# Feed-forward up projections as Strassen's seven block products, with the residual stream kept in DRAM meanwhile

## The chip, the cores and the metric

The kernel is one launch on one core of a Trainium2 chip. The metric is the device time of the launch in microseconds (us). A core has TensorE (PE in the profile, with its weight loads as PEld), VectorE (DVE), ScalarE (ACT), GpSimd (POOL) and SyncE (SP), which here issues nearly all DMAs. Each engine takes its instructions in the order in which they stand in its own queue; semaphores tie the queues together.

## The reference, cut to what matters

768 tokens (512 of one request, 256 of another) pass through two layers. Each layer is a mixer, a gated convolutional feed-forward and a gated embedding, each behind a root-mean-square norm and added to the residual `h`. The change is in the feed-forward:

```python
D_MODEL, D_FF, CONV_W = 1024, 2816, 3

def _rmsnorm(x, g):
    return x * lax.rsqrt(jnp.mean(x * x, axis=-1, keepdims=True) + EPS) * g

def _conv_ffn(x, w_up, conv_w, conv_b, w_down):
    u = x @ w_up                                   # (tokens, 2 * D_FF)
    up = jnp.pad(u, ((0, 0), (1, 1), (0, 0)))      # neighbours in the token direction
    u = up[:, :-2] * conv_w[0] + up[:, 1:-1] * conv_w[1] + up[:, 2:] * conv_w[2] + conv_b
    a, gate = jnp.split(u, 2, axis=-1)
    return (a * jax.nn.gelu(gate, approximate=False)) @ w_down

    # per layer l, in _trunk:
    h = h + _conv_ffn(_rmsnorm(h, norm_ffn_g[l]), ffn_w_up[l], ffn_conv_w[l], ffn_conv_b[l], ffn_w_down[l])
```

The arithmetic is float32.

## The kernel before

Features lie on the 128 partitions and tokens on the free axis. The residual is eight tiles `h0` to `h7` of 128 features by 768 tokens. A product of float32 quality is made of three float32r matmuls: weights and activations are each split into a high part and a low part (`whi`, `wlo`; `xh`, `xl`), and high by high, high by low and low by high are summed in PSUM (`gemm`, L78 to L85). Each of the three runs twice with the same weights, over the 512 tokens of one request and the 256 of the other.

Weights come in slabs of 128 x 1024 floats (512 KB), one for each 128 output features. `prep` (L58) loads a slab from DRAM on SP's queue (L66), makes the high part on ACT (L67) and the low part on DVE (L68). There are two buffers each of `raw`, `whi` and `wlo`, and `slab` keeps one slab ahead.

The feed-forward (`ffn`, L815) has 22 rounds j, one for each 128 of the 2816 features. A round has two projections (`proj`, L87), the value part and the gate part, of 24 pairs of matmuls each. DVE takes a projection out of PSUM and multiplies it by the norm's row factor `R` (L834), so the products run on the not yet normalized stream times the gain. Then the three taps of the convolution (ACT L838, DVE L839 and L841), the Gelu on ACT (L144), and the product into `act[j]` on DVE (L844). The first projection runs before `R` is there; the row sums follow it on PE (`proj0`, `norm_rows`). After the 22 rounds the down projection takes `act[j]` as its input (L131, L132, L85) and adds its sums to `h` (L865).

The order on each queue is made by the framework's scheduler from the order of the program and from priorities. Where a tile's buffer is used again, the new writer waits for the readers of the old.

## Time and profile before

| | |
|---|---|
| median of 3 runs | 2372.55 us (2371.6 to 2372.74) |
| span of the profiled execution | 2371.5 us |
| PE busy | 2347.3 us, 99% of the span |
| DVE busy | 1332.5 us, 56% |
| ACT busy | 918.7 us, 39% |
| POOL busy | 49.8 us, 2% |
| DVE's first L834 (round 0 of the first layer) | at 717.3 us |
| stretch of rounds 2 to 21 of the first layer in the rows below | 736.4 to 1072.2 us |

The profiled execution's span lies 1 us under the median, so the sums in span and the metric can be taken as one scale. PE's busy share alone does not say that PE is at its peak: matmuls overlap in it, and their ends are modelled. The distance from one start to the next is what counts. The idle time in a group's line is that of its engine, and what ended it.

### The profile page before, as it was taken

To read this page: it belongs to the slowest core of one execution; us is meant where nothing else is said; L and a number is where in the kernel's file an instruction comes from. 1 tells how busy PE (TensorE), PEld (TensorE's weight loads), DVE (VectorE), ACT (ScalarE), POOL (GpSimd) and SP (SyncE) were. 2 spreads that over 40 slices of the span, in tenths; PEclk is the share of its full clock that TensorE was granted. 3 is DMA by queue.
4 is the path that set the end of the run, shared out by engine and by line. 5 is a ranking of instruction groups with operands and counts; after the bars stand their busy time and mean duration, and the time that the engine had idled before them with its cause. 6 is when DMAs were issued, how large, how long until landed. Compare 5 with 4: busy or idle time off the path is not lost.

```text
span 2371.5 us, 32752 instructions
## 1 busy us (share of the span) xinstructions
PE 2347.3 (99%) x14004; PEld 2074.1 (87%) x14004; DVE 1332.5 (56%) x1814; ACT 918.7 (39%) x1190; POOL 49.8 (2%) x82
## 2 busy tenths in 40 slices
...
DMA packets 45616, 153.09 MB, mean 65 GB/s; under 512 B 5184, under 2 KB 7232, under 8 KB 45472
## 3 DMA queue, kind: packets, MB, share of 16 engines
...
q14 instruction: 34, 0.28, 0.0%
...
## 4 chain that ended last, share of the span: by engine, by line
PE 97%; DVE 1%; ACT 0%; issue 0%; DMA 0%; POOL 0%; SPq 0%; DVEq 0%
PE pj L85 76%; PE mm L85 11%; PE mm L249 4%; PE mm L331 2%; PE mm L692 1%; PE mm L299 1%; PE mm L235 1%; PE mm L553 0%; PE mm L609 0%; PE mm L685 0%; DVE y L934 0%; PE mm L212 0%; PE mm L290 0%; PE mm L344 0%; DMA xin<-xT 0%
## 5 line engine op out<-in xcount | busy, mean ns | idle before, releaser
L85 PE MATMUL pj<-xh,whi 128*128 128x512 f32 x3440 | 905.8, 344 | 8.9 <-ACT whi L67 5.8
L85 PE MATMUL pj<-xl,whi 128*128 128x512 f32 x3440 | 881.8, 337 | 2.5 <-DVE xl L138 2.4
L85 PE MATMUL pj<-xh,wlo 128*128 128x512 f32 x3440 | 879.4, 337 | 0.0
L85 PEld LDWEIGHTS pj<-xl,whi 128*128 128x128 f32 x3440 | 530.9, 188 | 80.7 <-DVE xl L138 4.6
L85 PEld LDWEIGHTS pj<-xh,whi 128*128 128x128 f32 x3440 | 527.6, 189 | 77.3 <-ACT whi L67 5.8
L85 PEld LDWEIGHTS pj<-xh,wlo 128*128 128x128 f32 x3440 | 525.8, 188 | 75.5
L67 ACT ACTIVATE whi<-raw 128x1024 fp32r<-128x1024 f32 (+1 forms) x244 | 255.8, 1048 | 761.0 <-PE pj L85 753.4
L68 DVE TENSOR_TENSOR wlo<-raw,whi 128x1024 fp32r<-128x1024 f32 (+1 forms) x244 | 296.8, 1216 | 139.2 <-ACT whi L67 139.1
L834 DVE TENSOR_TENSOR u<-pj,R 128x512 f32<-128x512 f32 (+1 forms) x176 | 90.1, 554 | 261.3 <-PE pj L85 261.1
L132 DVE TENSOR_TENSOR xl<-act,xh 128x770 fp32r<-128x770 f32 x88 | 83.5, 956 | 72.7 <-ACT xh L131 72.7
L131 ACT ACTIVATE xh<-act 128x770 fp32r<-128x770 f32 x88 | 73.7, 842 | 96.1 <-PE pj L85 96.1
L262 ACT COPY kc<-X 128x768 f32<-128x768 f32 x56 | 50.4, 900 | 124.5 <-PE mm L249 65.0
L85 PE MATMUL mm<-xh,whi 128*128 128x512 f32 x352 | 90.8, 339 | 0.0
L85 PE MATMUL mm<-xh,wlo 128*128 128x512 f32 x352 | 90.4, 338 | 0.0
L85 PE MATMUL mm<-xl,whi 128*128 128x512 f32 x352 | 90.4, 338 | 0.0
L249 PE MATMUL mm<-qc,kc 128*128 128x128 f32 x672 | 84.1, 275 | 0.0
L249 PEld LDWEIGHTS mm<-qc,kc 128*128 128x128 f32 x672 | 79.9, 192 | 2.2
L277 DVE COPY_PREDICATED A<-masks,mm 128x512 f32<-128x512 uint8 x112 | 60.4, 586 | 36.4 <-PE mm L249 36.3
L266 DVE TENSOR_TENSOR X<-X,F 128x768 f32<-128x768 f32 x56 | 53.4, 953 | 37.0 <-ACT qc L262 30.2
L144 ACT ACTIVATE cg<-cg 128x770 f32<-128x770 f32 x44 | 37.4, 849 | 89.1 <-DVE cg L841 89.1
L844 DVE TENSOR_TENSOR act<-act,cg 128x770 f32<-128x770 f32 x44 | 42.3, 961 | 38.5 <-ACT cg L144 38.5
L85 PEld LDWEIGHTS mm<-xh,whi 128*128 128x128 f32 x352 | 54.5, 189 | 7.5
...
## 6 DMA issues: line engine op xcount, KB each, us to landing
raw<-w_up SPq DMA_DIRECT2D x88, 512.0 KB, 3.5
raw<-w_ev SPq DMA_DIRECT2D x55, 512.0 KB, 3.5
raw<-w_dn SPq DMA_DIRECT2D x44, 512.0 KB, 3.5
raw<-w_od SPq DMA_DIRECT2D x24, 512.0 KB, 3.5
raw<-w_pg SPq DMA_DIRECT2D x16, 512.0 KB, 3.5
raw<-w_evo SPq DMA_DIRECT2D x8, 512.0 KB, 3.5
raw<-w_odo SPq DMA_DIRECT2D x8, 512.0 KB, 3.5
xin<-xT SPq DMA_DIRECT2D x8, 384.0 KB, 6.1
```

Of the source, the lines that this page charges most:

```text
L67: nc.scalar.activation(hi[:, s], raw[:, s], AF.Copy)
L68: nc.vector.tensor_tensor(out=lo[:, s], in0=raw[:, s], in1=hi[:, s].bitcast(F32), op=ALU.subtract)
L85: nc.tensor.matmul(o, w, x[:, c0:c0 + n], start=first and si == 0, stop=last and si == 2)
L131: nc.scalar.activation(xh[:, :n], src, AF.Copy)
L132: nc.vector.tensor_tensor(out=xl[:, :n], in0=src, in1=xh[:, :n].bitcast(F32), op=ALU.subtract)
L249: nc.tensor.matmul(p[:, j * 128:(j + 1) * 128], k[:, i * 128:(i + 1) * 128], q[:, i * 128:(i + 1) * 128], start=True, stop=True)
L262: nc.scalar.copy(dst.rearrange("p (n c j) -> p n c j", c=2, j=h), src)
L266: nc.vector.tensor_tensor(out=v1[:, :, 1, :], in0=v1[:, :, 1, :], in1=fv[:, :, 0, 0:1].to_broadcast([128, 2 * nb, h]), op=ALU.mult)
L277: nc.vector.copy_predicated(A[:, tl[0]:tl[0] + n, :], self.masks[:, li, :].unsqueeze(1).to_broadcast([128, n, 128]), p.rearrange("p (i t) ...
L331: nc.tensor.matmul(oo, l, r, start=n == 0, stop=n == len(mms) - 1)
L834: nc.vector.tensor_tensor(out=u[:, 1 + uc:1 + uc + w], in0=pj[:, c0:c0 + w], in1=self.R[:, c0:c0 + w], op=ALU.mult)
L844: nc.vector.tensor_tensor(out=act[j], in0=act[j], in1=c, op=ALU.mult)
```

## The change

The up projections of rounds 0 and 1 stay as they were (`NSTD` = 2). Each of rounds 2 to 21 is made of Strassen's seven block products in Winograd's form, with 15 block additions. The two by two blocks are: for the weights, input-feature tiles in pairs (k = 2p, 2p + 1) by value and gate part; for the tokens, the same pairs of feature tiles by two halves of the token axis. The token axis is 512 + 4 + 256 = 772 columns wide, with a gap of four zeros between the requests, so that a half is 386 columns (`HC`). The seven products run over four pairs p each, three float32r matmuls to a pair: 7 x 4 x 3 = 84 matmuls of 386 columns a round, against 96 (48 of 512 and 48 of 256 columns) before.

What comes with it:
- `prep_pair`: the weights of a round arrive in two loads of 512 KB, `ra` and `rb`, which take both `raw` buffers. S1 and S3 are made on POOL, S2 and S4 on DVE, and the high and low parts of A11 and A12, S2 and S1, S3 and S4, and A22 on ACT and DVE: 3584 columns to split a round, against 2048.
- `seven_operands`, four times, one for each pair of feature tiles, in rounds 0 and 1: the tokens are normalized on DVE (with `R`, so that a round's sums need no further factor), T1 and T2 are made on DVE, T3 and T4 on POOL, and seven high and low parts on ACT and DVE. Some of the parts are kept in the buffers of `h0` to `h7`.
- Hence `h` is written to DRAM ahead of the feed-forward, and read back for the sum with the down projection.
- `seven`: the products P1 to P7 go to three PSUM banks x, y and z; the sums are made on ACT (copies), DVE (additions out of PSUM) and POOL (`g`).
- `us` has two buffers instead of three, the gate's `c` one instead of two. The norm's `xh` and `xl` lie in buffers of `act`, and the order of the buffers in the down projection differs.

```diff
-UC = 1 + TP + 2 + TS + 1
-AC = TP + 2 + TS
-ACOL = ((0, TP), (TP + 2, TS))
+GAP = 4
+UC = 1 + TP + GAP + TS + 1
+AC = TP + GAP + TS
+HC = AC // 2
+NSTD = 2
...
+        if n == 2048:
+            self.ready.append(self.prep_pair(src))
+            return
         raw = self.wp.tile([128, 1024], F32, tag="raw", name="raw")
...
 
+    def prep_pair(self, src):
+        nc = self.nc
+        ra = self.wp.tile([128, 1024], F32, tag="raw", name="ra")
+        nc.sync.dma_start(out=ra, in_=src[:, 0:1024])
+        rb = self.wp.tile([128, 1024], F32, tag="raw", name="rb")
+        nc.sync.dma_start(out=rb, in_=src[:, 1024:2048])
+        a11, a12, a22, a21 = ra[:, 0:512], ra[:, 512:1024], rb[:, 0:512], rb[:, 512:1024]
+        def parts(hpool, htag, lpool, ltag, r):
+            n = r.shape[-1]
+            hi = hpool.tile([128, 1024], F32R, tag=htag, bufs=2, name=htag)[:, :n]
+            lo = lpool.tile([128, 1024], F32R, tag=ltag, bufs=2, name=ltag)[:, :n]
+            nc.scalar.activation(hi, r, AF.Copy)
+            nc.vector.tensor_tensor(out=lo, in0=r, in1=hi.bitcast(F32), op=ALU.subtract)
+            return [[(hi[:, c:c + 128], lo[:, c:c + 128]) for c in range(c0, c0 + 512, 128)]
+                    for c0 in range(0, n, 512)]
+        sa = self.fp.tile([128, 1024], F32, tag="S", bufs=2, name="sa")
+        sb = self.fp.tile([128, 1024], F32, tag="S", bufs=2, name="sb")
+        s2, s1, s3, s4 = sa[:, 0:512], sa[:, 512:1024], sb[:, 0:512], sb[:, 512:1024]
+        nc.gpsimd.tensor_tensor(out=s1, in0=a21, in1=a22, op=ALU.add)
+        nc.gpsimd.tensor_tensor(out=s3, in0=a11, in1=a21, op=ALU.subtract)
+        nc.vector.tensor_tensor(out=s2, in0=s1, in1=a11, op=ALU.subtract)
+        nc.vector.tensor_tensor(out=s4, in0=a12, in1=s2, op=ALU.subtract)
+        w = {}
+        w["A11"], w["A12"] = parts(self.wp, "whi", self.wp, "wlo", ra)
+        w["S2"], w["S1"] = parts(self.fp, "hs", self.fp, "ls", sa)
+        w["S3"], w["S4"] = parts(self.fp, "hs", self.fp, "ls", sb)
+        w["A22"], = parts(self.wp, "whi", self.wp, "wlo", rb[:, 0:512])
+        return w
+    def seven(self, X, c11, add):
+        nc = self.nc
+        W = self.slab()
+        x, y, z = None, None, None
+        def prod(bank, a, b, start):
+            for n, ((wh, wl), (xh, xl)) in enumerate(zip(W[a], X[b])):
+                for i, (w, v) in enumerate(((wh, xh), (wh, xl), (wl, xh))):
+                    nc.tensor.matmul(bank, w, v, start=start and n == 0 and i == 0, stop=n == 3 and i == 2,
+                                     skip_group_check=True)
+            self.tick()
+        pt = self.rp.tile([128, AC], F32, tag="Rt", name="p15")
+        ug = self.rp.tile([128, AC], F32, tag="sq", name="ug")
+        p1, p5, u2, g = pt[:, 0:HC], pt[:, HC:AC], ug[:, 0:HC], ug[:, HC:AC]
+        x = self.mm()[:, 0:HC]
+        prod(x, "A11", "B11", True)
+        nc.scalar.copy(p1, x)
+        y = self.mm()[:, 0:HC]
+        prod(y, "S2", "T2", True)
+        nc.vector.tensor_tensor(out=u2, in0=y, in1=p1, op=ALU.add)
+        z = self.mm()[:, 0:HC]
+        prod(z, "S1", "T1", True)
+        nc.scalar.copy(p5, z)
+        nc.gpsimd.tensor_tensor(out=g, in0=p1, in1=p5, op=ALU.add)
+        prod(x, "A12", "B21", False)
+        c11(x)
+        prod(y, "S3", "T3", False)
+        add(1, 1, y, g)
+        prod(z, "S4", "B22", False)
+        add(0, 1, z, u2)
+        prod(y, "A22", "T4", False)
+        add(1, 0, y, p1)
+    def seven_operands(self, x1, x2, ta, tb, slots):
+        nc = self.nc
+        b11, b12, b21, b22 = x1[:, 0:HC], x1[:, HC:AC], x2[:, 0:HC], x2[:, HC:AC]
+        t1, t2, t3, t4 = ta[:, 0:HC], ta[:, HC:AC], tb[:, 0:HC], tb[:, HC:AC]
+        nc.vector.tensor_tensor(out=t1, in0=b12, in1=b11, op=ALU.subtract)
+        nc.gpsimd.tensor_tensor(out=t3, in0=b22, in1=b12, op=ALU.subtract)
+        nc.vector.tensor_tensor(out=t2, in0=b22, in1=t1, op=ALU.subtract)
+        nc.gpsimd.tensor_tensor(out=t4, in0=b21, in1=t2, op=ALU.subtract)
+        s11, h2, l2, ha, la, hb, lb = slots
+        for hi, lo, v in ((s11[:, 0:HC], s11[:, HC:AC], b11), (ha, la, ta), (h2, l2, x2), (hb, lb, tb)):
+            nc.scalar.activation(hi, v, AF.Copy)
+            nc.vector.tensor_tensor(out=lo, in0=v, in1=hi.bitcast(F32), op=ALU.subtract)
+        self.X["B11"].append((s11[:, 0:HC], s11[:, HC:AC]))
+        for names, h, lo in ((("B21", "B22"), h2, l2), (("T1", "T2"), ha, la), (("T3", "T4"), hb, lb)):
+            self.X[names[0]].append((h[:, 0:HC], lo[:, 0:HC]))
+            self.X[names[1]].append((h[:, HC:AC], lo[:, HC:AC]))
...
     def ffn(self, l):
         nc, tc, a = self.nc, self.tc, self.a
-        with tc.tile_pool(name=f"f{l}", bufs=1) as fp:
+        with tc.tile_pool(name=f"f{l}", bufs=1) as fp, \
+                tc.tile_pool(name=f"hd{l}", bufs=1, space=bass.MemoryType.DRAM) as dp:
+            self.fp = fp
             conv = fp.tile([128, 2 * NF, 4], F32, tag="conv", name="conv")
             nc.sync.dma_start(out=conv, in_=a["conv"][l])
-            us = [fp.tile([128, UC], F32, tag=f"u{i}", name=f"u{i}") for i in range(3)]
-            self.norm_split(lambda k: self.h[k], C_FFN + 8 * l)
+            us = [fp.tile([128, UC], F32, tag=f"u{i}", name=f"u{i}") for i in range(2)]
+            def aslot(j, name, dt=F32R):
+                return fp.tile([128, AC], dt, tag=f"act{j}", name=name)
+            self.norm_split(lambda k: self.h[k], C_FFN + 8 * l, slot=lambda i, n: aslot(6 + i, n))
+            hd = dp.tile([KT, 128, T], F32, tag="hd", name="hd")
+            for k in range(KT):
+                nc.sync.dma_start(out=hd[k], in_=self.h[k])
             for u in us:
                 nc.gpsimd.memset(u[:, 0:1], 0.0)
-                nc.gpsimd.memset(u[:, 1 + TP:3 + TP], 0.0)
+                nc.gpsimd.memset(u[:, 1 + TP:1 + TP + GAP], 0.0)
                 nc.gpsimd.memset(u[:, UC - 1:UC], 0.0)
-            act = [fp.tile([128, AC], F32, tag=f"act{j}", name=f"act{j}") for j in range(NF)]
-            n = 0
-            for j in range(NF):
-                for part in range(2):
-                    pj = self.proj0(split=True) if n == 0 else self.proj()
-                    u = us[n % 3]
-                    n += 1
+            act = [None] * NF
+            self.X = {n: [] for n in ("B11", "B21", "B22", "T1", "T2", "T3", "T4")}
+            def operands(p):
+                x1, x2 = aslot(2, f"xn{2 * p}", F32), aslot(3, f"xn{2 * p + 1}", F32)
+                for k, x in ((2 * p, x1), (2 * p + 1, x2)):
+                    nc.gpsimd.memset(x[:, TP:TP + GAP], 0.0)
                     for (c0, w), (uc, _) in zip(CH, ACOL):
-                        nc.vector.tensor_tensor(out=u[:, 1 + uc:1 + uc + w], in0=pj[:, c0:c0 + w],
-                                                in1=self.R[:, c0:c0 + w], op=ALU.mult)
...
+                        nc.vector.scalar_tensor_tensor(out=x[:, uc:uc + w], in0=self.h[k][:, c0:c0 + w],
+                                                       scalar=self.cols[:, C_FFN + 8 * l + k:C_FFN + 8 * l + k + 1],
+                                                       in1=self.R[:, c0:c0 + w], op0=ALU.mult, op1=ALU.mult)
+                tags = [(self.xp, f"x{p}"), (fp, f"xb{p}")] + [(self.xp, f"x{4 + 3 * p + i}") for i in range(3)] \
+                    + [(self.hp, f"h{2 * p + i}") for i in range(2)]
+                self.seven_operands(x1, x2, aslot(4, "ta", F32), aslot(5, "tb", F32),
+                                    [pool.tile([128, AC], F32R, tag=t, name=t) for pool, t in tags])
+            def conv_taps(c, u, f):
...
+            def activate(j, u):
+                act[j] = aslot(j, f"act{j}", F32)
+                c = fp.tile([128, AC], F32, tag="c", name="cg")
+                conv_taps(act[j], u[0], j)
+                conv_taps(c, u[1], NF + j)
                 self.other(c, c, AF.Gelu)
                 nc.vector.tensor_tensor(out=act[j], in0=act[j], in1=c, op=ALU.mult)
+            for j in range(NSTD):
+                for part in range(2):
+                    n = 2 * j + part
+                    pj = self.proj0(split=True) if n == 0 else self.proj()
+                    for (c0, w), (uc, _) in zip(CH, ACOL):
+                        nc.vector.tensor_tensor(out=us[part][:, 1 + uc:1 + uc + w], in0=pj[:, c0:c0 + w],
+                                                in1=self.R[:, c0:c0 + w], op=ALU.mult)
+                    if part == 1:
+                        activate(j, us)
+                    operands(n)
+            for j in range(NSTD, NF):
+                u = us
+                def add(m, half, bank, other):
+                    o = u[m][:, 1 + half * HC:1 + (half + 1) * HC]
+                    nc.vector.tensor_tensor(out=o, in0=bank, in1=other, op=ALU.add)
+                    if half:
+                        nc.gpsimd.memset(u[m][:, 1 + TP:1 + TP + GAP], 0.0)
+                self.seven(self.X, lambda bank: nc.scalar.copy(u[0][:, 1:1 + HC], bank), add)
+                activate(j, u)
             self.use_lnexp()
             for ph in range(2):
                 accs = []
-                    xh, xl = self.split(j % 8, act[j])
+                    xh, xl = self.split((0, 1, 4, 5, 6, 7, 2, 3)[j % 8], act[j])
                     for m in range(4):
                         c = ((j % 2) * 4 + m) * 128
                         self.gemm(accs[m], hi[:, c:c + 128], lo[:, c:c + 128], xh, xl, ACOL, j == 0, j == NF - 1)
                 for m in range(4):
-                    h = self.h[ph * 4 + m]
+                    h = self.hp.tile([128, T], F32, tag=f"h{ph * 4 + m}", name=f"h{ph * 4 + m}")
+                    self.h[ph * 4 + m] = h
+                    nc.sync.dma_start(out=h, in_=hd[ph * 4 + m])
                     for o, (c0, w) in zip(accs[m], CH):
                         nc.vector.tensor_tensor(out=h[:, c0:c0 + w], in0=h[:, c0:c0 + w], in1=o, op=ALU.add)
                     self.square(ph * 4 + m, h)
 
...
-            for j in range(NF):
+            for j in range(NSTD):
                 r += [a["w_up"][l, j], a["w_up"][l, NF + j]]
+            r += [a["w_up2"][l, j] for j in range(NSTD, NF)]
```

How the queues stand. First DVE in a round in the middle of the up projections, before (two projections, value and gate part):

```order
L834 TENSOR_TENSOR u_5825<-pj,R 128x512
L834 TENSOR_TENSOR u_5825<-pj,R 128x256
L68 TENSOR_TENSOR wlo<-raw,whi 128x1024
L839 SCALAR_TENSOR_TENSOR act_5878<-u_5825,conv,act_5878 128x770
L841 SCALAR_TENSOR_TENSOR act_5878<-u_5825,conv,act_5878 128x770
L834 TENSOR_TENSOR u_5826<-pj,R 128x512
L834 TENSOR_TENSOR u_5826<-pj,R 128x256
L68 TENSOR_TENSOR wlo<-raw,whi 128x1024
L839 SCALAR_TENSOR_TENSOR cg<-u_5826,conv,cg 128x770
L841 SCALAR_TENSOR_TENSOR cg<-u_5826,conv,cg 128x770
L844 TENSOR_TENSOR act_5878<-act_5878,cg 128x770
```

The same place now, DVE in a round of seven products. `ug` holds P1 + P2 and then P1 + P5; `sa` is S2 and S1, `sb` S3 and S4 of the next round, `ls` their low parts, `ra` and `rb` the next round's raw weights, `mm` a PSUM bank, `u_5827` and `u_5828` the value and the gate part:

```order
L130 TENSOR_TENSOR ug<-mm,p_6576 128x386
L99 TENSOR_TENSOR sa<-sa,ra 128x512
L959 TENSOR_TENSOR act_6540<-act_6540,cg 128x772
L100 TENSOR_TENSOR sb<-ra,sa 128x512
L91 TENSOR_TENSOR ls<-sa,hs 128x1024
L91 TENSOR_TENSOR wlo<-ra,whi 128x1024
L975 TENSOR_TENSOR u_5828<-mm,ug 128x386
L975 TENSOR_TENSOR u_5827<-mm,ug 128x386
L91 TENSOR_TENSOR ls<-sb,hs 128x1024
L948 SCALAR_TENSOR_TENSOR act_6675<-u_5827,conv,act_6675 128x772
L91 TENSOR_TENSOR wlo<-rb,whi 128x512
L975 TENSOR_TENSOR u_5828<-mm,p_6576 128x386
```

Three taps (L950, L948, L950) follow and close the round: 15 instructions instead of 11, and the sums for PE's banks (L130, L975) now stand between the next round's weights.

POOL, which had nothing to do in the up projections, in a round of seven products:

```order
L97 TENSOR_TENSOR sa<-rb 128x512
L98 TENSOR_TENSOR sb<-ra,rb 128x512
L134 TENSOR_TENSOR ug<-p_6711 128x386
L977 MEMSET u_5828 128x4
L977 MEMSET u_5827 128x4
```

S1 and S3 of the next round, then g = P1 + P5 of this one, then the gaps.

DVE in the first layer's round 0, before, around the low part of the weights of the fourth projection (`wlo_6036`; `pj_5977` is the second projection):

```order
L834 TENSOR_TENSOR u0_5825<-pj_5897,R_5956 128x512
L834 TENSOR_TENSOR u0_5825<-pj_5897,R_5956 128x256
L839 SCALAR_TENSOR_TENSOR act0_5869<-u0_5825,conv_5823,act0_5869 128x770
L834 TENSOR_TENSOR u1_5826<-pj_5977,R_5956 128x512
L841 SCALAR_TENSOR_TENSOR act0_5869<-u0_5825,conv_5823,act0_5869 128x770
L834 TENSOR_TENSOR u1_5826<-pj_5977,R_5956 128x256
L68 TENSOR_TENSOR wlo_6036<-raw_6034,whi_6035 128x1024
```

And now: the same low part is `wlo_6080`, and 28 instructions stand between the first L965 (the former L834) and it; the last of them, it, and the next:

```order
L152 TENSOR_TENSOR ta_6057<-xn3_6050,ta_6057 128x386
L959 TENSOR_TENSOR act0_6039<-act0_6039,cg_6040 128x772
L157 TENSOR_TENSOR x7_6061<-xn3_6050,xb1_6060 128x772
L157 TENSOR_TENSOR x9_6063<-ta_6057,x8_6062 128x772
L157 TENSOR_TENSOR h3_6065<-tb_6058,h2_6064 128x772
L74 TENSOR_TENSOR wlo_6080<-raw_6078,whi_6079 128x1024
L965 TENSOR_TENSOR u0_5827<-pj_6084,R_5941 128x512
```

`xn` is a normalized pair of tiles, `ta` T1 and T2, `tb` T3 and T4; the L157 rows are low parts of operands of pairs 0 and 1. The low part moved from the 7th place behind `R` to the 30th. The operands of pairs 2 and 3 (rows of the same kind, and the first `prep_pair`) follow it.

## Rows read from the trace of the kernel before

**Rows 1.** The page's busy time by engine, share and instructions.

```profile
PE 2347.3 (99%) x14004; PEld 2074.1 (87%) x14004; DVE 1332.5 (56%) x1814; ACT 918.7 (39%) x1190; POOL 49.8 (2%) x82
```

**Rows 2.** The page's chain that ended last, by line.

```profile
PE pj L85 76%; PE mm L85 11%; PE mm L249 4%; PE mm L331 2%; PE mm L692 1%; PE mm L299 1%; PE mm L235 1%; PE mm L553 0%; PE mm L609 0%; PE mm L685 0%; DVE y L934 0%; PE mm L212 0%; PE mm L290 0%; PE mm L344 0%; DMA xin<-xT 0%
```

**Rows 3.** DVE by line, rounds 2 to 21, layer 0 (busy us, mean ns, idle before).

```profile
L68 DVE TENSOR_TENSOR wlo<-raw,whi 128x1024 fp32r<-128x1024 f32 x40 | 48.6, 1215 | 0.1
L834 DVE TENSOR_TENSOR u<-pj,R 128x512 f32<-128x512 f32 x80 | 40.9, 554 | 129.6 <-PE pj L85 129.6
```

**Rows 4.** DVE and ACT in order of time in mid-layer: start us, us, instruction, idle.

```profile
921.29 1.02 DVE L834 TENSOR_TENSOR u<-pj,R 128x512 f32<-128x512 f32 x2 [4.18 <-PE pj L85]
922.23 1.22 DVE L68 TENSOR_TENSOR wlo<-raw,whi 128x1024 fp32r<-128x1024 f32 x1
922.34 1.04 ACT L838 ACTIVATE cg<-u,conv 128x770 f32<-128x770 f32 x1 [0.28 <-DVE u L834]
...
938.06 1.02 DVE L834 TENSOR_TENSOR u<-pj,R 128x512 f32<-128x512 f32 x2 [4.18 <-PE pj L85]
```

**Rows 5.** PE in order of time where only 512-column matmuls follow each other.

```profile
2295.43 0.40 PE L85 MATMUL mm<-xh,ghi 128*128 128x512 f32 x1
...
2296.12 0.40 PE L85 MATMUL mm<-xh,ghi 128*128 128x512 f32 x1
```

**Rows 6.** DVE in order of time, instructions that do not wait for each other.

```profile
695.06 1.22 DVE L68 TENSOR_TENSOR wlo<-raw,whi 128x1024 fp32r<-128x1024 f32 x1
696.19 0.95 DVE L196 TENSOR_TENSOR acc<-acc,sq 128x768 f32<-128x768 f32 x1
697.06 5.66 DVE L138 SCALAR_TENSOR_TENSOR xl<-h,cols,xh 128x768 fp32r<-128x768 f32 x6
...
1069.54 2.70 DVE L132 TENSOR_TENSOR xl<-act,xh 128x770 fp32r<-128x770 f32 x3
```

**Rows 7.** DVE, then POOL, in order of time at the start; POOL alone later.

```profile
8.04 1.02 DVE L138 SCALAR_TENSOR_TENSOR xl<-xin,cols,xh 128x768 fp32r<-128x768 f32 x1 [1.20 <-ACT xh L137]
8.98 0.42 DVE L68 TENSOR_TENSOR wlo<-raw,whi 128x256 fp32r<-128x256 f32 x1
9.91 2.00 DVE L138 SCALAR_TENSOR_TENSOR xl<-xin,cols,xh 128x768 fp32r<-128x768 f32 x1 [0.52 <-ACT xh L137]
11.83 2.03 DVE L68 TENSOR_TENSOR wlo<-raw,whi 128x256 fp32r<-128x256 f32 x1
...
9.14 8.48 POOL L196 TENSOR_TENSOR acc<-acc,sq 128x768 f32<-128x768 f32 x4 [7.61 <-ACT sq L195]
...
43.00 1.85 POOL L471 TENSOR_TENSOR ks<-X 128x768 f32<-128x768 f32 x1 [25.37 <-DVE X L466]
```

**Rows 8.** DMA issues by line: count, KB each, us from issue to landing.

```profile
raw<-w_up SPq DMA_DIRECT2D x88, 512.0 KB, 3.5
...
hd<-h SPq DMA_DIRECT2D x8, 384.0 KB, 2.8
h<-hd SPq DMA_DIRECT2D x8, 384.0 KB, 3.5
```

**Rows 9.** ACT by line, rounds 2 to 21 of layer 0 (columns as in Rows 3).

```profile
L67 ACT ACTIVATE whi<-raw 128x1024 fp32r<-128x1024 f32 x41 | 43.5, 1062 | 180.4 <-PE pj L85 180.4
```

**Rows 10.** DVE, then ACT, in order of time, first rounds of layer 0.

```profile
716.19 0.96 DVE L169 TENSOR_TENSOR R<-R,Rt 128x768 f32<-128x768 f32 x1
...
719.67 1.06 ACT L67 ACTIVATE whi<-raw 128x1024 fp32r<-128x1024 f32 x1 [0.27 <-PE pj L85]
...
728.05 1.06 ACT L67 ACTIVATE whi<-raw 128x1024 fp32r<-128x1024 f32 x1 [1.54 <-PE pj L85]
```

**Rows 11.** Stretches at the start: us, busy us by engine, granted clock, DMA.

```profile
20.00:25.00 5.00, 5.00 (x17) 4.23 (x17) 5.00 (x6) 0.84 (x1) 0.00 (x0) 0.50 0.82 268
25.00:40.00 15.00, 15.00 (x84) 12.78 (x83) 9.84 (x14) 7.79 (x10) 0.00 (x0) 1.00 0.49 179
```

More of the change, by code (lines that the diff above doesn't have):

```diff
@@ L122, in mm, with xslot, split @@
         return self.ps.tile([128, 512], F32, tag="mm", bufs=4, name="mm")
-    def split(self, k, src, gain=None, dve=False):
+    def xslot(self, i, name, dt=F32R):
+        return self.xp.tile([128, AC], dt, tag=f"x{i}", name=name)
+    def split(self, k, src, gain=None, dve=False, slot=None):
         nc = self.nc
         n = src.shape[-1]
-        xh = self.xp.tile([128, AC], F32R, tag=f"xh{k}", name=f"xh{k}")
-        xl = self.xp.tile([128, AC], F32R, tag=f"xl{k}", name=f"xl{k}")
+        slot = slot or self.xslot
+        xh, xl = slot(2 * k, f"xh{k}"), slot(2 * k + 1, f"xl{k}")
         if gain is None:
@@ L170, in rsqrt_rows, with norm_split @@
                                                           op=ALU.mult).ins)
-    def norm_split(self, get, gcol, share=()):
+    def norm_split(self, get, gcol, share=(), slot=None):
         self.xh, self.xl = [], []
         for k in range(KT):
-            xh, xl = self.split(k, get(k), self.cols[:, gcol + k:gcol + k + 1], k in share)
+            xh, xl = self.split(k, get(k), self.cols[:, gcol + k:gcol + k + 1], k in share, slot)
             self.xh.append(xh)
@@ new lines, in conv_taps @@
+            def conv_taps(c, u, f):
+                nc.scalar.activation(c, u[:, 1:1 + AC], AF.Identity, scale=conv[:, f, 1:2], bias=conv[:, f, 3:4])
+                nc.vector.scalar_tensor_tensor(out=c, in0=u[:, 0:AC], scalar=conv[:, f, 0:1], in1=c, op0=ALU.mult,
+                                               op1=ALU.add)
+                nc.vector.scalar_tensor_tensor(out=c, in0=u[:, 2:2 + AC], scalar=conv[:, f, 2:3], in1=c,
+                                               op0=ALU.mult, op1=ALU.add)
```

14 lines of the change are left out of this document (6 added, 8 removed).

## The prediction

> **What bounds the kernel now.** The page's busy times come first: PE is busy for 99% of the span, DVE for 56%, ACT for 39% and POOL for 2% [rows 1]. The chain that ended last then tells whether that matters: PE's lines make nearly all of it, 76% of the span in L85's projections alone, and no transfer stands in it [rows 2]. Grouping DVE by line over rounds 2 to 21 of the first layer shows the room beside PE: its 80 takings from PSUM wait 129.6 us for PE, 6.5 us a round [rows 3]. A round lasts 16.77 us, from one value part's taking at 921.29 to the next at 938.06 [rows 4]; DVE works 10.3 of them. So PE's columns set the time, and what shortens PE here counts until DVE, POOL or the weights' path is late.
>
> **PE's part of the change.** A round before is 48 pairs of 512 and 256 columns, so a pair costs 16.77 / 48 = 0.349 us. Where 512 columns stand alone, three starts lie 0.69 us apart [rows 5]: 0.230 each, which leaves 0.119 for 256. No row has 386 columns; on the line between the two they cost 0.119 + 130/256 x 0.111 = 0.175. The bounds are 0.119 and 0.230; 386 lies in the middle, and nothing in the rows suggests a step. 84 of them make 14.73 us, 2.04 less than before. Over 20 rounds and two layers that is 81 us, 3.4%: the most that the change can bring.
>
> **DVE in a round of seven.** Instructions that don't wait for each other start closer together than they last: 1.13 us for 1024 columns (695.06 to 696.19), (5.66 - 1.01) / 5 = 0.93 for a tap of 768, (2.70 - 0.95) / 2 = 0.87 for 770 without a scalar [rows 6], 0.94 for 512 and 256 out of PSUM (921.29 to 922.23) [rows 4], so 0.47 for 386. A sum of 512 in SBUF lies between 0.42 (256 columns) [rows 7] and 1.22 (1024), 0.69, or 0.60 when overlapped like the others. The round's 15 instructions are 4 out of PSUM (1.9), 3 of 512 (1.8), 3 low parts of 1024 (3.4), 4 taps (3.7) and the Gelu's product (0.9): 11.7 us. Alone this would fit into 14.73.
>
> **POOL beside DVE.** POOL's 768-column sum lasts 1.85 alone, so by proportion 1.23 for S1 and for S3 and 0.93 for g. At the start POOL adds four times in 8.48 us from 9.14 on. Until then DVE's L138 took 1.02 and its 256-column L68 0.42; beside it they take 2.00 and 2.03 [rows 7]. Both read two operands from SBUF, as POOL does: the one waits until the other is through. Of DVE's 15 new instructions 11 read two operands from SBUF; the four out of PSUM read one there.
>
> The Trainium skill's "SBUF — State Buffer" ("Who interferes with whom") says that a DVE instruction with two SBUF inputs and a GpSimd one that reads SBUF exclude each other for a whole instruction. By that rule work given to POOL here is no relief for DVE; the trace agrees with 2.03 for 0.42 us.
>
> **The path that sets a round.** Both `raw` buffers are taken by one round, and the second load can't be issued before the low part of A22 (`wlo` from `rb`) is made, which itself waits for P7 of the round before to be through with the old A22. From there, in the order of the queues: that low part 0.69; the load 3.5 [rows 8]; S1 1.23 and S3 1.23 on POOL; S2 0.60; g on POOL 0.93, with DVE shut out; the Gelu's product 0.87; S4 0.60; low parts of S2 and S1, and of A11 and A12, 1.13 each; the sum of bank y (first L975) 0.47, for which P7 waits on PE since it goes on in y; P7 itself 12 x 0.175 = 2.10; the high part of A22 on ACT, a little over half of 1.06 [rows 9], 0.60; and then the low part again. That is 15.1 us. Six hand-offs between queues of 0.03 each (DVE ends at 922.31, ACT starts at 922.34 [rows 4]) add 0.2: **15.3 us a round**, 0.6 above PE's own 14.73, 1.47 below the old round. What is queued behind the waiting S2 is the whole of DVE's round, and P7 waits for that. Bounds: 14.73 if nothing of POOL's falls on the path; 16.3 with POOL's sums as long as beside DVE (8.48 / 4 = 2.12 for 768: 0.5 more) and DVE's six steps not overlapping (0.09 each: 0.5 more).
>
> **The start of a layer.** R is there at 717.15 [rows 10]. All operands need R and DVE. Up to the last low part of B11, which P1 of round 2 needs for its last quarter, DVE has: 4 takings 3.8; 16 normalizing pieces, eight tiles of about 1.0, 8.1; 11 pieces of 386 at 0.47, 5.2; 9 low parts of 772, 7.8; 8 taps 7.4 and 2 products 1.7; one slab's low part 1.1; the first `prep_pair` 5.2. Sum 40.3 us. ACT's high parts, which some of them wait for, add some 2.5. POOL's 7 T sums and 4 S sums are 11.4 us; I let 7 of them stand in DVE's way, the rest beside PSUM reads and waits. So this low part is done at about 717.15 + 50 = 767. PE, which ended projections at 719.67 and 728.05 [rows 10], would be through with the fourth at 736.4. It is not: that slab's low part moved to place 30 on DVE, some 22 us behind R, so the fourth projection ends near 748; this is covered by the longer wait. After 767 come P1's last 0.5, then P2 waits for the last low part of T1 and T2 (a sum, a low part, S2 of the next round and this one, 3.6 with POOL) until 770.6, then 0.5 and five products of 2.10: 781.6. Before, round 2 ended at 728.05 + 3 x 8.385 = 753.2. Loss 28.4 us. And PE has stood still for over 10 us: at the kernel's start, after waits, it was busy from 20 to 25 us at a granted clock of 0.50, that is 1.2 GHz, and at 1.00 behind it [rows 11]; half of 5 us is 2.5. **Loss 31 us a layer**, bounds 23 (nothing shut out by POOL: 43 us instead of 50) and 36 (all 11.4 in the way).
>
> **What costs nothing.** The eight writes of h (384 KB, 2.8 us to land [rows 8]) are issued one after each output projection, 8 us apart, and the buffers are written again only after R. The reads (3.5) have the whole down projection as cover; without it the first would cost 3.5 and PE's next half would wait. The end of round 21 has no next pair to prepare, and the first down-projection operands are split during P4 to P7. ACT has 8 us of work in a round. The mixers' and gates' queues keep their order.
>
> **The sum.** A layer: 31.0 lost, then 19 rounds x 1.47 = 27.9 won, 3.1 net loss. Two layers: 6 us, so a span of 2377.7 and, 1 us above, **2378.5 us**. The balance turns where 19 rounds win 31 us, at 15.14 us a round.
>
> **Rivals.** *PE keeps the pace* (faster). If POOL's sums mostly fall into DVE's waits (for the load, for PE), a round lasts 14.73 and the start loses 23: 23 - 19 x 2.04 = -15.8 a layer, 2341 us. For it: DVE's own 11.7 us leave 3 us free, near the 3.4 of POOL. Against: S1, S3 and g stand right between the load's landing and DVE's run up to P7, not in its idle time. *The loop is longer than PE by more* (slower). At 16.3 us a round and 36 lost, it is 36 - 19 x 0.47 = 27 a layer, 2426 us; the place is P7 waiting for the first L975, and from 15.14 us a round on it loses. For it: beside DVE, POOL took 2.12 instead of 1.85. Against: overlap on DVE shows in all of rows 6. *386 columns cost as much as 512*, so that the products do not shorten PE: 84 x 0.230 = 19.3 a round, 2.5 more, with the start 2 x (31 + 49) = 160 us slower, 2532. Only the missing row speaks for it.
>
> **How the numbers follow.** Forecast 0.50, PE's pace 0.31, the longer loop 0.17, the dear columns 0.02. The forecast's own range, 15.3 by 0.4 either way, is 2362 to 2395. About 0.2% (4.7 us) is what a measurement of this kernel can tell from no change. Of the forecast's 0.50, 0.07 is faster by more, 0.16 within, 0.27 slower. With the rivals: faster 0.38, same 0.16, slower 0.46. The range of 8 in 10 goes from 2340, half-way into the first rival, to 2415, most of the way to the second.
>
> **What would show it.** PE's starts of 386 columns 0.175 apart; a round of 15.3 us with 0.6 of PE idle ahead of P7, ended by DVE's L975; DVE's instructions with two SBUF inputs lengthened beside POOL's L97, L98 and L134; PE idle for some 12 us ahead of the fourth projection and over 15 us ahead of round 2's products, ended by DVE's L74 and L157; a granted clock of 0.50 behind that. The prediction is wrong if a round runs at 14.7 us without PE idle, if the start loses under 23 us, or if a new wait shows at the down projection.

## The result, and the profile after

| | before | after |
|---|---|---|
| median (lowest to highest), us | 2372.36 (2371.60 to 2372.74) | 2385.89 (2384.81 to 2386.94) |
| ratio, 95% interval | | 1.0058 (1.0044 to 1.0073) |
| span of the profiled execution, us | 2371.5 | 2384.8 |
| layer 0: PE starts what follows round 2, round 21 | 753.35, 1072.05 | 785.22, 1081.56 |
| layer 1: PE starts what follows round 2, round 21 | 1767.89, 2086.59 | 1806.84, 2101.16 |

The change makes the kernel 0.58% slower, 13.5 us, and the interval leaves out 1. The forecast was 2378.5 us, 6 us slower than before, with a range of 2340 to 2415 and "slower" at 0.46: the direction was right, and the loss is more than twice the forecast's. The last two lines of the table show where the time went. The first round of products ends 31.9 us late in layer 0 and 29.4 in layer 1 (38.95, less the 9.51 brought along from layer 0); the 19 rounds behind it win 22.4 and 24.4 back. So the layers lose 9.5 and 5.1 us.

The page of the changed kernel, busy times and the chain that ended last, answers to [rows 1, 2]:

```profile
PE 2291.9 (96%) x13524; PEld 2083.2 (87%) x13524; DVE 1571.4 (66%) x2054; ACT 1052.1 (44%) x1422; POOL 247.6 (10%) x308
...
PE 13%; DVE 5%; DMA 3%; issue 2%; POOL 1%; ACT 1%; DVEq 0%; POOLq 0%
PE mm L177 7%; PE pj L177 4%; DMA rb<-w_up 3%; PE mm L119 3%; DVE wlo L91 1%; DVE sa L99 1%; POOL sa L97 1%; DVE sb L100 1%; ACT whi L90 0%; DVE u L975 0%; DVE y L1071 0%; DVE ls L91 0%; PE mm L307 0%; DVE z L1095 0%; DVE acc L291 0%
```

PE's busy time fell by 55 us, but the time in which it stands idle grew by 69, from 24 us (2371.5 - 2347.3) to 93 (2384.8 - 2291.9); the difference is the 13 us lost. The chain names what PE waits behind: the load of `rb`, DVE's L91, L99 and L100, POOL's L97, and L975, one after the other. It reaches back from the end of the kernel only to 1796 us, so it shows the rounds of layer 1 and what follows them; its shares add up to a quarter of the span. Before, it reached over nearly the whole span, and only lines of PE had a share that doesn't round to nothing.

One round of products in layer 0, first DVE, then POOL, then SyncE, then PE; in brackets the idle time ahead and what ended it:

```profile
926.53 0.69 DVE L91 TENSOR_TENSOR wlo<-rb,whi 128x512 fp32r<-128x512 f32 x1 [0.18 <-ACT whi L90]
...
932.37 1.75 DVE L99 TENSOR_TENSOR sa<-sa,ra 128x512 f32<-128x512 f32 x1 [1.03 <-POOL sa L97]
934.04 1.63 DVE L959 TENSOR_TENSOR act<-act,cg 128x772 f32<-128x772 f32 x1
935.59 0.68 DVE L100 TENSOR_TENSOR sb<-ra,sa 128x512 f32<-128x512 f32 x1
...
938.47 1.02 DVE L975 TENSOR_TENSOR u<-mm,ug 128x386 f32<-128x386 f32 x2
...
941.97 0.69 DVE L91 TENSOR_TENSOR wlo<-rb,whi 128x512 fp32r<-128x512 f32 x1
...
931.04 1.30 POOL L97 TENSOR_TENSOR sa<-rb 128x512 f32<-128x512 f32 x1 [6.81 <-DMA rb<-w_up]
932.29 1.28 POOL L98 TENSOR_TENSOR sb<-ra,rb 128x512 f32<-128x512 f32 x1
933.53 1.32 POOL L134 TENSOR_TENSOR ug<-p 128x386 f32<-128x386 f32 x1
...
927.25 0.33 SPq L83 DMA_DIRECT2D rb<-w_up  x1
...
923.59 0.63 PE L119 MATMUL mm<-h,whi 128*128 128x386 f32 x2 [0.86 <-DVE u L975]
```

It reads as a ring, from one low part of A22 to the next: 926.53, end 927.22; the load issued at 927.25; POOL's S1 from 931.04, S3 to 933.53; S2, g and the Gelu's product in turn to 935.59; S4 and two low parts to 938.47; L975 to 939.03; P7, then A22's high part, to 941.97: 15.44 us. DVE's L99, a sum of 512 columns, lasts 1.75 beside POOL's L98, and L959 1.63 beside L134; the same kind of sum, L100, lasts 0.68 when POOL is quiet. PE's row is of the round before: it waits for L975 ahead of P7, as in all 18 rounds between the first and the last of a layer, for 0.1 to 1.7 us.

That this ring sets the rounds can be read from the trace: from one low part of A22 to the next, less the time from the issue of `rb`'s load to POOL's start, it takes 11.65 to 11.74 us in each of 35 rings in the two layers, while that one link takes 3.53 to 5.13 (3.88 in the mean). The longest of these links, POOL and then SyncE:

```profile
1009.63 1.29 POOL L97 TENSOR_TENSOR sa<-rb 128x512 f32<-128x512 f32 x1 [8.14 <-DMA rb<-w_up]
...
1004.49 0.33 SPq L83 DMA_DIRECT2D rb<-w_up  x1
```

The start of layer 0 in order of time, PE, then POOL, then DVE:

```profile
742.46 1.01 PE L177 MATMUL pj<-xh,wlo 128*128 128x512 f32 x2 [11.01 <-DVE wlo L74]
...
770.34 0.69 PE L119 MATMUL mm<-x,whi 128*128 128x386 f32 x1 [7.88 <-DVE x L157]
...
733.69 4.72 POOL L151 TENSOR_TENSOR tb<-xn,xn 128x386 f32<-128x386 f32 x1 [8.07 <-DVE xn L938]
...
738.52 0.87 POOL L153 TENSOR_TENSOR tb<-xn,ta 128x386 f32<-128x386 f32 x1
...
736.59 0.96 DVE L157 TENSOR_TENSOR x<-ta,x 128x772 fp32r<-128x772 f32 x1
740.30 0.96 DVE L157 TENSOR_TENSOR h<-tb,h 128x772 fp32r<-128x772 f32 x1 [2.75 <-ACT h L156]
741.18 1.22 DVE L74 TENSOR_TENSOR wlo<-raw,whi 128x1024 fp32r<-128x1024 f32 x1
```

PE waits 11 us for the fourth projection's low part and 8 for the last low part of B11. The table by windows (us, busy us of PE, PEld, DVE, ACT, POOL, granted clock, DMA share, GB/s), of the fourth projection, of what follows that low part of B11, and of what follows the products of layer 0:

```profile
742.46:752.58 10.12, 10.12 (x44) 8.72 (x44) 7.96 (x12) 3.30 (x5) 6.88 (x6) 0.73 0.17 52
...
770.34:780.00 9.66, 8.29 (x27) 7.27 (x28) 6.82 (x9) 4.63 (x7) 3.06 (x2) 0.57 0.00 2
...
1081.56:1420.00 338.44, 338.44 (x1962) 295.60 (x1962) 188.16 (x218) 154.03 (x192) 0.00 (x0) 1.00 0.24 83
```

In the last stretch, which begins with the down projection and the read-back of h, PE has no gap.

### The profile page after: what moved, and what is told of

The parts are those of the page before. It is cut to its first block, busy times and chain, and to the rows that moved or that the text cites. A ratio compares the mean times of both kernels' runs of the same rounds, so it can differ in the third digit from the quotient of the medians.

```text
span 2384.8 us, 32943 instructions
## 1 busy us (share of the span) xinstructions
PE 2291.9 (96%) x13524; PEld 2083.2 (87%) x13524; DVE 1571.4 (66%) x2054; ACT 1052.1 (44%) x1422; POOL 247.6 (10%) x308
## 5 line engine op out<-in xcount | busy, mean ns | idle before, releaser
L177 PE MATMUL pj<-xh,whi 128*128 128x512 f32 (+1 forms) x2160 | 576.8, 348 | 9.2 <-ACT whi L73 6.1
L177 PE MATMUL pj<-xh,wlo 128*128 128x512 f32 (+1 forms) x2160 | 555.8, 339 | 22.0 <-DVE wlo L74 22.0
L177 PE MATMUL pj<-xl,whi 128*128 128x512 f32 (+1 forms) x2160 | 556.1, 338 | 2.7 <-DVE xl L233 2.7
L177 PEld LDWEIGHTS pj<-xh,wlo 128*128 128x128 f32 (+1 forms) x2160 | 331.6, 189 | 70.7 <-DVE wlo L74 22.7
L177 PEld LDWEIGHTS pj<-xl,whi 128*128 128x128 f32 (+1 forms) x2160 | 333.3, 189 | 52.6 <-DVE xl L233 4.5
L177 PEld LDWEIGHTS pj<-xh,whi 128*128 128x128 f32 (+1 forms) x2160 | 333.5, 190 | 50.7 <-ACT whi L73 6.1
L119 PE MATMUL mm<-x,hs 128*128 128x386 f32 x800 | 221.7, 342 | 4.5 <-ACT hs L90 3.7
L119 PE MATMUL mm<-x,whi 128*128 128x386 f32 x480 | 139.8, 345 | 20.2 <-DVE x L157 15.8
L119 PEld LDWEIGHTS mm<-x,hs 128*128 128x128 f32 x800 | 147.9, 190 | 6.1 <-ACT hs L90 4.4
L119 PE MATMUL mm<-x,ls 128*128 128x386 f32 x320 | 109.5, 342 | 0.0
L99 DVE TENSOR_TENSOR sa<-sa,ra 128x512 f32<-128x512 f32 x40 | 69.7, 1743 | 44.2 <-POOL sa L97 44.2
```

Of the source, the lines that this page charges most:

```text
L99: nc.vector.tensor_tensor(out=s2, in0=s1, in1=a11, op=ALU.subtract)
L119: nc.tensor.matmul(bank, w, v, start=start and n == 0 and i == 0, stop=n == 3 and i == 2, skip_group_check=True)
L177: nc.tensor.matmul(o, w, x[:, c0:c0 + n], start=first and si == 0, stop=last and si == 2)
```

## The experiments

Line numbers move by a few lines where a kernel has lines added. "First seven" is the end of layer 0's first round of products. P1 to P7 are the products in PE's order; the kernel's `p5` and the P5 in the sum P1 + P5 are the third of them.

**1. The sums of a round on DVE.**

```diff
-        nc.gpsimd.tensor_tensor(out=s1, in0=a21, in1=a22, op=ALU.add)
+        nc.vector.tensor_tensor(out=s1, in0=a21, in1=a22, op=ALU.add)
```

and the same for `s3` and `g`.

> S1, S3 and g move from POOL to DVE; nothing else. Theory (a round is the loop from the low part of A22 through the load, POOL's two sums with DVE shut out, and P7): in the trace of the changed kernel that loop reads 0.69 + 3.82 + 2.49 + 2.06 + 0.60 + 2.28 + 0.56 + 2.27 + 0.67 = 15.4 us. With three sums of about 0.6, 0.6 and 0.47 on DVE it is 0.69 + 3.82 + 1.2 + 0.6 + 0.87 + 0.6 + 2.28 + 0.56 + 2.27 + 0.67 = 13.6, so PE's own 84 x 0.177 = 14.85 sets the round: no idle time of PE ahead of P7, 19 x (15.55 - 14.85) x 2 = 26 us less, 2359 us (2355 to 2364). Rival (DVE is simply too busy: 14.0 of 15.6 us): three more instructions of together 1.7 us make a round of 17.2 and 2386 + 38 x 1.7 = 2450 us.

Measured: 2369.72 us, ratio to before 0.9988 (0.9978 to 0.9997); rounds of 15.17 and 15.10. The rival falls: more work on DVE made the round shorter. But the pace of PE is not reached. DVE and SyncE in order of time:

```profile
910.19 0.69 DVE L97 TENSOR_TENSOR sa<-rb 128x512 f32<-128x512 f32 x1
...
912.28 0.68 DVE L99 TENSOR_TENSOR sa<-sa,ra 128x512 f32<-128x512 f32 x1
912.88 0.55 DVE L130 TENSOR_TENSOR ug<-mm,p 128x386 f32<-128x386 f32 x1
...
906.42 0.33 SPq L83 DMA_DIRECT2D rb<-w_up  x1
```

And from the waits in these rounds of layer 0 (total us, times, longest):

```profile
PEld mm L119 <- DVE ug L130: 7.0, 16, 1.2
```

The scheduler, with other costs on DVE, put L130 behind S2. L130 needs only PE, but now it waits for the load; P5, the fifth product, which goes on in the bank that L130 reads, waits for it. The expectation summed the ring in the old order.

**2. The same, with POOL's sums made again for nobody.**

```diff
+        nc.gpsimd.tensor_tensor(out=dm, in0=a21, in1=a22, op=ALU.add)
+        nc.gpsimd.tensor_tensor(out=dm, in0=a11, in1=a21, op=ALU.subtract)
...
+        nc.gpsimd.tensor_tensor(out=dm[:, 0:HC], in0=p1, in1=p5, op=ALU.add)
```

> As the run before, and POOL makes the same three sums again into a buffer that nothing reads (the temporary of the convolution lies in R's place, to make room for it). No result on any path waits for POOL now. Theory (POOL's sum of two SBUF tiles and a DVE instruction with two SBUF operands shut each other out): POOL's 1.25 + 1.25 + 0.93 = 3.4 us are taken out of DVE's time; DVE has 11.7 + 1.7 = 13.4 us of its own, so 16.8 if none of it falls into DVE's waits: a round of 15.5 to 16.8, and 2385 to 2433 us. Rival (POOL was only slow as a link of the path, not in DVE's way): a round of 14.85 and 2359 us, as without the dummies.

Measured: 2512.53 us, ratio 1.0593 (1.0577 to 1.0609). DVE by line over the rounds of layer 0 (busy us, mean ns), here and then in experiment 1:

```profile
L964 DVE TENSOR_TENSOR act<-act,cg 128x772 f32<-128x772 f32 x18 | 36.3, 2014 | 0.0
L98 DVE TENSOR_TENSOR sb<-ra,rb 128x512 f32<-128x512 f32 x18 | 32.1, 1783 | 0.0
L99 DVE TENSOR_TENSOR sa<-sa,ra 128x512 f32<-128x512 f32 x18 | 23.7, 1314 | 0.0
```

```profile
L959 DVE TENSOR_TENSOR act<-act,cg 128x772 f32<-128x772 f32 x18 | 17.2, 956 | 0.0
L98 DVE TENSOR_TENSOR sb<-ra,rb 128x512 f32<-128x512 f32 x18 | 12.3, 686 | 0.0
L99 DVE TENSOR_TENSOR sa<-sa,ra 128x512 f32<-128x512 f32 x18 | 12.3, 685 | 0.0
```

The three lengthen by 1.06 + 1.10 + 0.63 = 2.8 us, though nothing waits for POOL's results: exclusion is shown by itself. The theory's bound of 16.8 a round was too low all the same: the sums hit the very instructions that P5 waits for, so all 2.8 add to the 15.1 of experiment 1. In layer 0 every second round lasts these 17.9; the others last 19.6. PE stands still for 3 us in each, and in every second one the granted clock is at its lower level (1.2 GHz) for part of the time behind it, as two windows of such a round show (columns as above); why not in the others is not shown:

```profile
911.85:915.00 3.15, 3.10 (x13) 3.10 (x14) 3.15 (x4) 1.93 (x3) 0.00 (x0) 0.72 0.02 5
915.00:920.00 5.00, 5.00 (x26) 5.00 (x25) 2.50 (x5) 2.25 (x3) 0.21 (x2) 0.83 0.30 105
```

**3. A third buffer for raw weights, sums on POOL.**

```diff
-        rb = self.wp.tile([128, 1024], F32, tag="raw", name="rb")
+        rb = self.wp.tile([128, 1024], F32, tag="raw", name="rb", bufs=3)
```

> A third buffer for raw weights; the sums stay on POOL (the temporary of the convolution lies in R's place, to make room). The second half of the next pair is now loaded once the low parts of A11 and A12 are made, some 4 us earlier, and no longer behind P7. Theory (the loop through the load and P7 sets the round): the loop is cut, the round falls to PE's 14.85 or to DVE's own 11.7 + 3.4 shut out = 15.1 at most, so 17 to 26 us less: 2360 to 2369 us. Rival (the loss is DVE's time, its own work and what POOL takes of it, and the load has nothing to do with it): a round of 15.5 and 2386 us.

Measured: 2381.22 us, ratio 1.0038 (1.0023 to 1.0053); rounds of 15.24 and 15.27. The window over 18 rounds of layer 0:

```profile
786.73:1061.51 274.78, 271.84 (x1514) 265.76 (x1514) 257.52 (x272) 135.31 (x180) 91.42 (x90) 1.00 0.21 70
```

One of POOL's waits in it (125.0 us in the changed kernel, longest 8.1), then two of DVE's:

```profile
POOL sa L97 <- DMA rb<-w_up: 46.4, 18, 2.9
...
DVE act L959 <- ACT cg L239: 8.0, 18, 0.4
...
DVE ls L91 <- ACT hs L90: 7.7, 19, 0.4
```

The load is early and the ring is cut, yet only 0.3 us of the 0.7 above PE's pace goes. DVE is busy 257.5 / 18 = 14.3 us a round, POOL's share included, and waits 0.9 for ACT: together 15.2. Under the ring lies a second limit, almost as high: DVE's queue, filled by being shut out. Neither theory nor rival alone is right. The two starts are 1.5 and 3.1 us longer than in the changed kernel, so that the time falls by 4.7 us only, not by the 11 of the rounds; why they are longer is not shown (the convolution's temporary lies in another buffer here).

**4. T3 and T4 on DVE.** The diff is as in 1, for `t3` and `t4`.

> T3 and T4, eight sums in each layer's start, move from POOL to DVE; the rounds stay as they are. Theory (the start is DVE's chain, POOL's sums stand in it): eight sums of 0.47 add 3.8 us to DVE, and POOL's times in the start (3.0 + 1.4, 4.7 + 0.9, 3.0 + 1.3, 1.6 + 1.5, which last up to four times their 0.93 since each waits for DVE) and DVE's waits of 1.6 and 2.8 for them go: 3 us less a layer (0 to 6), 2380 us (2374 to 2386), with the first seven products ending near 782 instead of 785.2. Rival (POOL's sums lie beside DVE's work there, so moving them only lengthens DVE's chain): 3.8 us more a layer, 2393 us.

Measured: 2375.65 us, ratio 1.0015 (1.0005 to 1.0024): 10 us less than the changed kernel. The first seven end at 778.1 instead of 785.2, and layer 1's start is 5 us shorter. POOL's relief costs DVE more here than it saves.

**5. The fourth projection's low part early.**

```diff
+                with self.tc.high_priority():
+                    nc.vector.tensor_tensor(out=lo[:, s], in0=raw[:, s], in1=hi[:, s].bitcast(F32), op=ALU.subtract)
```

> In the projections before the products, DVE makes the low parts of the weights at once: the fourth projection's moves from the 30th place behind R to the 8th. Theory (the prediction's: the fourth projection's wait is covered, since round 2 waits longer for DVE's chain of operands, whose sum doesn't change): the 11.35 us of idle PE ahead of the fourth projection go, and come back ahead of round 2's products; the first seven products still end near 785 (783 to 786), 2386 us (2382 to 2387; the little less if PE stands still in one stretch instead of two and its clock falls once). Rival (the two waits add up): 2 x 11.35 less, 2363 us.

Measured: 2386.87 us, ratio 1.0059 (1.0041 to 1.0077). PE in order of time:

```profile
753.37 1.65 PE L124 MATMUL mm<-x,hs 128*128 128x386 f32 x4 [16.11 <-ACT hs L95]
...
769.44 0.69 PE L124 MATMUL mm<-x,whi 128*128 128x386 f32 x1 [7.88 <-DVE x L162]
```

The 11 us ahead of the projection are gone and stand as 16 ahead of the products; the first seven end at 784.7. The wait was covered.

**6 and 7. Both limits of a round taken away.** Experiment 6 is 1 and 3 together. Experiment 7 is 1 with L130 raised:

```diff
+        with self.tc.high_priority():
+            nc.vector.tensor_tensor(out=u2, in0=y, in1=p1, op=ALU.add)
```

> All sums of a round on DVE, and the third raw buffer: POOL is out of DVE's way and the loop through the load is cut. With the sums on DVE alone a round lasts 15.14, and PE waits 0.2 to 0.4 ahead of P5 for DVE's L130, which stands behind L97, L98, L959 and L99 there, which wait for the load: 0.69 + 3.8 + 2.7 + 0.55 + 6.4 (P5 to P7) + 0.65 + hand-offs = 15.1. Theory (that loop): with the load early a round is PE's 14.85, 38 x 0.29 = 11 us less than 2370, 2359 us (2356 to 2363). Rival (DVE, busy 13.8 of 15.14, with its waits for ACT in between, is full): a round of 15.1 and 2369 us.

> All sums of a round on DVE, two raw buffers, and L130 (u2 = y + P1) ahead of the sums that wait for the load. Theory: P5 no longer waits for L130. The loop through the load goes on through DVE to the first L975 and P7 again: 0.69 + 3.8 + 0.6 + 0.87 + 0.6 + 0.6 + 0.47 + 0.6 + 2.28 + 0.5 + 2.27 + 0.67 = 13.95, below PE's 14.85: 11 us less than 2370, 2359 us (2356 to 2363). Rival (DVE is full): a round of 15.1 and 2369 us.

Measured: 2358.10 us, ratio 0.9940 (0.9924 to 0.9955), and 2359.75, ratio 0.9945 (0.9930 to 0.9961). 18 rounds of layer 0 in experiment 6:

```profile
782.57:1049.94 267.37, 267.37 (x1514) 267.37 (x1514) 245.54 (x325) 137.91 (x180) 3.72 (x36) 1.00 0.21 72
```

PE is busy in all 267.37 us: 14.85 a round. It is the same in experiment 7, whose edit differs from that of experiment 1 only in raising L130, with 14.84 a round:

```profile
784.74:1051.90 267.16, 267.16 (x1514) 267.06 (x1514) 248.27 (x325) 139.96 (x180) 3.72 (x36) 1.00 0.22 72
```

DVE's 13.6 us (experiment 6) and 13.8 (7) fit beneath, as long as nothing that PE waits for stands behind a load in DVE's queue. What is left against PE's pace is the start alone.

**8 and 9. Four rounds of projections before the products.** Experiment 8 is 7 with T3 and T4 on DVE and `NSTD = 4`, with one pair of operands in every second projection; experiment 9 is the changed kernel with `NSTD = 4` and the operands spread in the same way. In both some temporaries of the operands lie in other buffers.

```diff
-NSTD = 2
+NSTD = 4
...
-                    operands(n)
+                    if n in (0, 2, 4, 6):
+                        operands((0, 2, 4, 6).index(n))
```

> As e7, T3 and T4 on DVE too, and four rounds of projections before the products instead of two, one pair of operands with every second projection. Theory (the start is DVE's chain from R on, 7.0 us for each pair, and a round of projections leaves DVE 8 us free): PE's fourth round of projections ends near 770; by then DVE has about 52.5 us behind R at 717.6, to the last low part of B11 at 770; the first sums and low parts of the weights follow until about 777, so PE waits some 7 us once instead of 31: about 20 us less a layer than with two rounds and a pace of 14.85 (two more rounds at 16.77 counted), 2319 us (2310 to 2335). Rival (DVE's chain is as late, since the two added rounds bring it 8.8 us of their own each): the wait shrinks by 16 us only, of which 3.8 go into the slower rounds: 2335 to 2345 us.

> The changed kernel with four rounds of projections before the products instead of two, one pair of operands with every second projection, and nothing else: all sums stay on POOL as they were. Theory (the start is a chain of DVE work that two rounds of projections are too short for): the first seven products would end near 799, some 7 later than with POOL's sums on DVE (791.9), where the kernel before stands at 786.7 at this round; 17 rounds of 15.55 follow: 2322 + 2 x (7 + 17 x 0.6) = 2356 us (2348 to 2366). Rival (the start's loss isn't a matter of how long PE has other work): two more rounds of 16.77 instead of 15.55 a layer, 2386 + 5 = 2391 us.

Measured: 2322.43 us, ratio 0.9790 (0.9772 to 0.9807), and 2356.64, ratio 0.9935 (0.9918 to 0.9952). Experiment 9's first seven end at 798.9; the kernel before is through with this round at 753.35 + 2 x 16.77 = 786.9 (I had 786.7). The loss of 31.9 has become 12.0, because the operands have two more rounds of projections to be made in. In experiment 8 they end at 791.9, 5.0 behind, and PE waits over 1 us only once in this start:

```profile
742.64 1.01 PE L178 MATMUL pj<-xh,wlo 128*128 128x512 f32 x2 [3.88 <-DVE wlo L74]
```

**10 to 12. Towards the best version.** Experiment 10 is 8 with the third raw buffer, the second sum out of bank y raised as L130 was, and the last pair of operands one projection earlier. Experiment 11 adds the early low parts of 5 to it; 12 is 10 with three rounds of projections.

> e8 with the third raw buffer and the second sum out of bank y ahead of the first out of bank z (the convolution's temporary lies in other buffers to make room). Theory: the rounds of 15.04 and 15.07, and the last of 16.49 that waits in P4, fall to PE's 14.85: 2 x (17 x 0.2) = 7 us less than 2322, 2315.5 us (2311 to 2320). Rival (the temporary's new buffers hold up the first products): 2322 us or more.

> e10, and the low parts of the weights in the projections made at once, as in e5. In e8 PE waits 4.16 us ahead of the third projection for DVE's low part; that wait goes. Theory (as in e5: the products wait for DVE's chain, which isn't shorter): 0 to 3 us less than e10, 2314 us (2311 to 2317). Rival (with four rounds DVE's chain is through before PE is, so the wait counts in full, with the clock behind it): 2 x 5 = 10 us less than e10, 2305 us.

> e10 with three rounds of projections. Theory (DVE's chain): a round fewer takes DVE's own 8.8 us out of it, so the last low part of B11 is made near 763.5 and the weights' near 771, while PE is through with projections at 757: PE waits some 10 us, twice, with the clock lost behind it; against e10 a round of 16.77 less 14.85 is won back: 2 x 7.5 = 15 us more than e10, 2330 us (2322 to 2340). Rival (PE's dearer rounds count more than the wait): 4 us less than e10, 2312 us.

Measured: 2321.18 us (ratio 0.9786, 0.9772 to 0.9801), 2314.50 (0.9757, 0.9743 to 0.9772) and 2323.79 (0.9795, 0.9781 to 0.9810). Rows of PE's start in experiment 10, then in 11:

```profile
739.88 1.01 PE L179 MATMUL pj<-xh,wlo 128*128 128x512 f32 x2 [3.89 <-DVE wlo L74]
770.91 0.62 PE L179 MATMUL pj<-xh,wlo 128*128 128x512 f32 x2 [2.24 <-DVE wlo L74]
```

```profile
774.91 0.45 PE L124 MATMUL mm<-x,hs 128*128 128x386 f32 x1 [4.16 <-ACT hs L95]
```

In 10 the rounds reach 14.83 and win 3.7 and 3.9 us a layer, as expected; but the starts are 1.6 and 4.0 longer than in 8, with the eighth projection now waiting too, so little over 1 us is left, and the expected 2315.5 is missed. Which of its edits makes the starts longer was not tested. In 11 those waits of 6.1 us go, 4.2 come back ahead of P2, and 6.7 are won over both layers: between theory (0 to 3) and rival (10). With four rounds DVE's chain and PE seem to be nearly even. With three rounds (12) the products hardly wait; PE waits 10 us once, ahead of a projection; I had summed two waits, and the loss against 10 is 2.6 instead of 15. Of all kernels run, 11 is the fastest: 2.4% below the kernel before, 3.0% below the changed one.

## Why the prediction was right, point by point

**PE's part** held. Starts of 386 columns follow each other by 0.177 us in the median (estimate 0.175), 14.87 a round instead of 14.73. In order of time:

```profile
920.63 0.34 PE L119 MATMUL mm<-x,hs 128*128 128x386 f32 x1
920.80 0.34 PE L119 MATMUL mm<-xb,ls 128*128 128x386 f32 x1
920.98 0.34 PE L119 MATMUL mm<-xb,hs 128*128 128x386 f32 x1
```

The rival of the dear columns is out.

**POOL beside DVE** held. The rule read from [rows 7] is what makes L99 1.75 and L959 1.63. The Trainium skill's "SBUF — State Buffer" ("Who interferes with whom") has the one that comes second wait out the other's whole instruction; experiment 2 agrees, with 1.78 for 0.69. L975 and L130, which take one operand from PSUM, keep their 0.55 in every kernel here; in the changed one 33 of them run at the same time as one of POOL's sums, and none takes more than 0.56.

**The path of a round** held in its order, and the size was off: 15.3 forecast, 15.44 in the round shown, 15.60 and 15.49 in the mean of 19. Term by term: the load took 3.82 from the low part's end to S1 instead of 3.5; L975 0.56 instead of 0.47; P7 and A22's high part 2.9 instead of 2.7; S2, g and the Gelu's product 2.06 instead of 2.40; the rest as said. The mean lies above the round shown because loads differ: in the longest round, 16.8, `rb` was issued at 1004.49 and POOL began at 1009.63, 1.3 later than usual, and the round is longer by as much. The prediction took the 3.5 of the kernel before for each load; in this ring the usual one took 3.8, and a few took over 4. Of the second limit, DVE's own queue at 15.2, which experiment 3 laid bare, the prediction had both parts (11.7 of DVE, 3.4 of POOL), but it never put them together as a limit.

**The start** held: 31.9 and 29.4 us, against 31. Two misses nearly cancel in it. The last low part of B11 is made at 770.3 (forecast 767) and the fourth projection ends at 752.6 (748); but PE did more of the round ahead of it than forecast (28 of the 84 matmuls start before 770.3, where the forecast had 18), so that 14.9 us follow instead of 17.1. So the expected wait of over 15 us ahead of the products shows as several, the longest 7.9. Behind them the granted clock was 0.57 from 770.34 to 780.00, at its lower level for most of that time, as forecast. That the fourth projection's delay is covered is confirmed by experiment 5. The granted clock was at its lower level (1.2 GHz) for part of the fourth projection, hence the 0.73, and 10.12 us for 44 of its 48 matmuls, where the rows of [rows 10] lie 8.38 apart; this, too, the later wait covers.

**What costs nothing** held. The writes of h took 2.3 us to land, the reads of h 5.7 and 6.2 in the two layers instead of the 3.5 of [rows 8], and PE had no gap in the down projection of layer 0.

**The sum.** Forecast: 31.0 - 27.9 = 3.1 a layer. Measured: 31.9 - 22.4 = 9.5 and 29.4 - 24.4 = 5.1 (unrounded), and 1.3 us are won behind the layers: 13.3 in the span. The mis-sized term is the round, and in it the load (3.9 us in the mean instead of 3.5; the other links together are 0.1 shorter than forecast): a quarter of a microsecond, 38 times, is 9 us, of which the starts and what follows the layers give 2 back, and so 2378.5 became 2385.9. With a break-even at 15.14 us a round, 0.16 below the forecast's 15.3 and within its own 0.4, the sign hung on it: that it came out slower was in part luck.

**The rivals.** "PE keeps the pace" was wrong for this kernel, for the reason given against it: S1, S3 and g stand between the load and P7. With these sums on DVE and the order or the buffer mended, its 14.8 us a round came true, and the time with the start's full cost was 2358. "The loop is longer by more" named the right place, P7 behind the first L975, and was too dear.
